# A two-block transformer step with 32 routed experts on one core: the experts' biases split into three bfloat16 parts over 128 partitions, and the gated part normalised later

## The chip, the core and the metric

The kernel runs on one core of a Trainium2 chip. A core has TensorE (matmuls, PE in the profile; its weight loads are PEld), VectorE (DVE), ScalarE (ACT), GpSimd (POOL) and SyncE (SP), which issues most of the loads from DRAM; 16 DMA engines move the data. ScalarE and GpSimd issue some loads too, in line with their other instructions. The metric is the device time of one execution in microseconds (us), the median of three runs, lower is better. [...]

## The reference

256 tokens of width 1024 go through two blocks. The first block mixes tokens (windowed attention beside a gated part), then routes each token to 4 of 32 experts; the second block mixes again and has a feed-forward part. What the change touches, cut down:

```python
def chunked_spatial_gating(u, g, ln_g, ln_b, w_s, b_s):
    u = gelu(u)
    g = layer_norm(gelu(g))            # per token and group of 64
    mixed = einsum('gts,bcsgd->bctgd', tril(w_s), g) + b_s
    return u * mixed
def token_mixer(...):
    q, k, v, u, g = split(x @ w_in + b_in)
    return concat([attention(q, k, v), chunked_spatial_gating(u, g, ...)]) @ w_out + b_out
def expert_block(xb, e):               # for each of 32 experts e
    gt = minimum(xb @ w_gate[e] + b_gate[e], 7)
    up = clip(xb @ w_up[e] + b_up[e], -7, 7)
    hid = gt * sigmoid(1.702 * gt) * (up + 1)
    return hid @ w_down[e] + b_down[e]
```

All data are float32. The gate, up and down weights of one expert are 1024 x 1024 each, so the experts have 402.7 MB of weights in all.

## The kernel before

The order of the instructions on each engine is the order in which the Python code writes them; each engine works through its own list and waits on semaphores.

`front` does the first block's mixer for two tiles of 128 tokens and the router. Its products are made from float32 values split into two parts (`pieces` and `pump` load a piece of a weight, cast its high part on ScalarE and subtract the low part on VectorE or GpSimd, by the letters of `FRONT_LOW`). The order on TensorE is: k, v and q; `scores` (attention scores, softmax on VectorE and ScalarE); four `gate_half` for the gated input; `trp(0)` (transposes of the softmaxed scores of group 0, which `normalise(0)` has divided by their sums: the half s=0 on VectorE, the half s=1 on GpSimd); the chunk `u_chunk(0)`; `trp(1)`, `trp(2)`; `u_chunk(1)` to `u_chunk(3)`, each of which fills one of three accumulator banks tagged `mm` and is evicted through an activation on ScalarE; then `pv` (scores times values, three times, into the same three banks), the gating product, and the output projection (`out_half`, columns 0 to 511 as `wo0` for both tiles in four slices, then `wo1`). The gated input is evicted into `gx`, its statistics go through VectorE, and it is normalised: tile 0 by two VectorE instructions, tile 1 by eight ScalarE activations of 64 columns. `cc` and `cb` fold the norm's bias into the router's logits: `cc` is copied out of two columns of small products, and one more small product makes `cb` of it.

`moe` works in capacity 64: an expert has 64 slots of gathered tokens, and experts go in pairs (`EB` = 2). `gate_up(e)` forms `pg` and `pu`, `[128, 512]` each: rows 0 to 63 are the 64 slots by output columns 0 to 511, rows 64 to 127 the same slots by columns 512 to 1023. So each matmul uses 64 of the array's 128 columns, and the two column halves are written alternately. The bias opens the accumulation as a product of its own: a column of the identity, broadcast to 64 columns, against `bgu`, in which the 32 gate biases lie on partitions 0 to 31 and the up biases on 32 to 63, so with 32 rows of the array, in float32:

```python
r = slice(32 * q, 32 * q + 32)
self.mm(p[64 * fh:64 * fh + 64, :], self.ident[r, 32 * q + e:32 * q + e + 1].to_broadcast([32, CAP]),
        self.bgu[r, fh * 512:(fh + 1) * 512], start=True, stop=False)
```

`product` then adds eight slices of 128 rows for both halves. `finish` runs the down product of the expert before. The weights come through nine buffers (`PAIRS`) of 2 MB, each half of one weight matrix; `fetch` issues the load into a buffer behind the product that read it last, and 18 loads of 1 MB are issued in the front already. At a pair's end TensorE transposes the gated one-hot `og`, which VectorE makes in `gates_of`.

Of the kernel before, what the change touches and what calls it, by code (L numbers as in the profile page):

```python
# [12 lines left out]
F32 = mybir.dt.float32  # L13
F32R = mybir.dt.float32r
BF = mybir.dt.bfloat16
I32 = mybir.dt.int32
AF = mybir.ActivationFunctionType
# [54 lines left out]
class Net:  # L72
# [66 lines left out]
    def run(self):  # L139
        nc, tc, ctx, a = self.nc, self.tc, self.ctx, self.a  # L140
        ctx.enter_context(tc.manual_schedule())
        self.cpool = ctx.enter_context(tc.tile_pool(name="consts", bufs=1))
        cp = self.cpool
        pa = self.pa = ctx.enter_context(tc.tile_pool(name="ring_a", bufs=1))
        bctx = ctx.enter_context(ExitStack())
        pb = self.pb = bctx.enter_context(tc.tile_pool(name="ring_b", bufs=1))

        self.x = cp.tile([128, NT, D], F32, name="x")
        for t in range(NT):
            nc.sync.dma_start(self.x[:, t, :], a["x"][0, t * 128:(t + 1) * 128, :])  # L150

        self.ident = cp.tile([128, 128], F32, name="ident")
        make_identity(nc, self.ident)
        self.h = cp.tile([128, NT, D], F32, name="h")
        self.lg = cp.tile([128, NT, NE], F32, name="lg")
        self.bgu = pb.tile([64, D], F32, name="bgu")

        self.ones = pb.tile([128, 96], F32, name="ones")
        nc.gpsimd.memset(self.ones, 1.0)
        self.bits = pb.tile([128, 2, 128], BF, name="bits")  # L160
        nc.gpsimd.memset(self.bits, 1.0)
        nc.gpsimd.affine_select(out=self.bits[:, 0], in_=self.bits[:, 0], compare_op=OP.is_ge, fill=0.0, base=-1,
                                pattern=[[1, 128]], channel_multiplier=-1)
        self.slot1 = pb.tile([128, CAP], F32, name="slot1")
        nc.gpsimd.iota(self.slot1, pattern=[[1, CAP]], base=1, channel_multiplier=0,
                       allow_small_or_imprecise_dtypes=True)
        self.top = pb.tile([128, NT, 8], F32, name="top")

        self.norm1 = pb.tile([128, 2, KC], F32, name="norm1")
        with ExitStack() as fctx:  # L170
            self.front(fctx)
        if self.stop == "front":
            return
        self.acc, self.h = self.h, self.x
        self.late = ctx.enter_context(tc.tile_pool(name="late", bufs=1, side="right", reuse_waits="tile"))
        with ExitStack() as mctx:
            sums = self.moe(mctx)
            if self.stop == "moe":
                for t in range(NT):
                    for n in range(2):  # L180
                        nc.vector.tensor_copy(self.acc[:, t, n * 512:(n + 1) * 512], sums[t][n])
                self.dump("acc", self.acc)
                return
            self.tail_norm(sums)
        bctx.close()
        with ExitStack() as tctx:
            self.mixer2(tctx)
        if self.stop == "mixer2":
            return
        self.ffn2()  # L190
# [9 lines left out]
    def front(self, fctx):  # L200
        nc, tc, a = self.nc, self.tc, self.a
        V, S, G = nc.vector, nc.scalar, nc.gpsimd
        fp = fctx.enter_context(tc.tile_pool(name="front", bufs=1))
        f2 = fctx.enter_context(tc.tile_pool(name="front2", bufs=2))
        ps = fctx.enter_context(tc.tile_pool(name="front_ps", bufs=1, space=PSUM, reuse_waits="tile"))

        def bank(tag, shape):
            return ps.tile(shape, F32, tag=tag, bufs={"mm": 3, "s": 4, "o": 1}[tag], name=self.nm(tag))
# [82 lines left out]
        def after_wo():  # L291
            L["wr"] = load("wr", [128, KC, NE], a["w_router"][0].rearrange("(k p) e -> p k e", p=128))
            L["br"] = load("br", [128, NE], bcast_rows(a["b_router"], NE))
            for q, nme in enumerate(("b_gate", "b_up")):
                nc.sync.dma_start(self.bgu[32 * q:32 * q + 32, :], a[nme][0])

        self.pieces(spec, halves, [slot[f"r{i}"] for i in range(9)])
        self.after = {0: after_kv, 2: after_q, 4: after_g, 7: after_wo}
# [165 lines left out]
        def u_chunk(c):  # L464
            S.activation(uT[:, c, :], channels("u"), AF.Gelu_apprx_tanh, bias=bqs[:, 6 + c:7 + c])

        for i in range(3):
            scores(i)

        r = self.h  # L470
        for t in range(NT):
            for n in range(2):
                ns = slice(n * 512, (n + 1) * 512)
                V.scalar_tensor_tensor(r[:, t, ns], self.x[:, t, ns], ALPHA, L["bout"][:, ns], op0=OP.mult, op1=OP.add)

        p = bank("s", [128, 4, 128])
        for gg in range(8):
# [25 lines left out]
        rs = self.rsqrt(fp, mv[:, :, 1], 16, add=1e-5)  # L503
        nb = fp.tile([128, 8], F32, name="gnb")
        V.scalar_tensor_tensor(nb, mv[:, 8:16, 0], -1.0, rs[:, 8:16], op0=OP.mult, op1=OP.mult)
        for j in range(8):
            S.activation(g[:, 8 + j, :], g[:, 8 + j, :], AF.Identity, scale=rs[:, 8 + j:9 + j], bias=nb[:, j:j + 1])
        gt = g[:, 0:8]
        V.tensor_tensor(gt, gt, mv[:, 0:8, 0:1].to_broadcast([128, 8, 64]), op=OP.subtract)
        V.tensor_tensor(gt, gt, rs[:, 0:8, None].to_broadcast([128, 8, 64]), op=OP.mult)  # L510

        u_chunk(1)
        u_chunk(2)
        u_chunk(3)
        xp = part_tiles()
        for i in range(3):
# [92 lines left out]
        for i in range(4):  # L609
            out_half(po, range(NT), i, self.parts("wo0"))  # L610
            freed()
        for t in range(NT):
            evict(t, 0, po[t])
        cc = fp.tile([128, 2], F32, name="cc")
        V.tensor_copy(cc[:, 0:1], by_experts("b", wr, lambda k: bqs[:, 10 + k:11 + k], 1))
        V.tensor_copy(cc[:, 1:2], by_experts("m", wrg, lambda k: self.ones[:, 0:1], 1))
        fac = {}
        p = bank("mm", [128, 512])
        for i in range(4):
            out_half({0: p}, (0,), i, self.parts("wo1", i))  # L620
            if i == 0:
                pc = bank("s", [128, 2, NE])
                for x in range(2):
                    self.mm(pc[:, x, :], cc[:, x:x + 1].to_broadcast([128, 128]), ist)
                V.tensor_tensor(cb[:, 0, :], pc[:, 0, :], L["br"], op=OP.add)
                V.tensor_copy(cb[:, 1, :], pc[:, 1, :])
            elif i > 1:
                turned(i - 2, 0, 4)
        evict(0, 1, p)
        fac[0] = norm(0)  # L630
# [76 lines left out]
    def moe(self, mctx):  # L707
# [141 lines left out]
        def gate_up(e, between=()):  # L849
            b, el = divmod(e, EB)  # L850
            pg, pu = bank("g", 2, [128, 512]), bank("u", 2, [128, 512])
            for q, (p, nme) in enumerate(((pg, "w_gate"), (pu, "w_up"))):
                for fh in range(2):
                    r = slice(32 * q, 32 * q + 32)
                    self.mm(p[64 * fh:64 * fh + 64, :], self.ident[r, 32 * q + e:32 * q + e + 1].to_broadcast([32, CAP]),
                            self.bgu[r, fh * 512:(fh + 1) * 512], start=True, stop=False)
                product(p, lambda k: xg[b][:, k, el * CAP:(el + 1) * CAP], weights_of(e, nme), False)
                for f in between if not q else ():
                    f()
            return swiglu(pg, pu)  # L860
# [1228 lines left out]
```

## Time and profile before

| | |
|---|---|
| median of three runs | 1596.21 us (1593.58 to 1598.78) |
| the profiled execution | 1599.51 us |
| its span, first to last instruction | 1597.9 us |
| mean granted clock | 0.962 |
| busy: TensorE, VectorE, ScalarE, GpSimd | 1491.1, 612.0, 374.6, 143.8 us |
| read from DRAM | 486.78 MB |

Busy times are unions of the instructions' spans. A float32 matmul leaves two records on TensorE, one for each half of its work; records overlap since matmuls are pipelined. An instruction's name gives the tile written, an arrow, and the tiles read. Line L89 is the helper that all matmuls go through, L1355 and L1356 the split of the weights.

### The profile page before, as it was taken

Reading aid. Unit: us, or ns where it says so; the run is one execution under the profiler, and the core shown is the slowest. Engines: PE = TensorE matmul, PEld = TensorE weight load, DVE = VectorE, ACT = ScalarE, POOL = GpSimd, SP = SyncE. Lnnn points to the kernel's source line nnn. Section 1 sums busy time; section 2 is a strip of 40 time slices with the busy share of each in tenths; the row PEclk is TensorE's granted clock in tenths of the full one; section 3 lists DMA queues with packets and bytes.
Section 4 is the critical chain, followed back from the end, with each engine's and each line's share of the span. In section 5 each row is a group of like instructions: output and inputs, shape, how many; then the busy total and the mean of one; then the engine's idle time right before and its main releaser. Section 6 shows DMA issues by size and latency. Waiting matters only on the chain. (4 is left out here: it accounts for less than half of the span.)

```text
span 1597.9 us, 19498 instructions
## 1 busy us (share of the span) xinstructions
PE 1491.1 (93%) x8102; PEld 832.1 (52%) x8102; DVE 612.0 (38%) x1138; ACT 374.6 (23%) x644; POOL 143.8 (9%) x140
## 2 busy tenths in 40 slices
PE   8889899999999998999999999997988899999998
PEld 7773233332332333332333333334877787799998
DVE  5852231221221212121211421215568556776664
ACT  4531110110101101111101111102634223355552
POOL 2200000000000002000000000003444214200000
PEclk9999889999999999999999999998999999999999
DMA  9769989999999999999999999981433124665540
GB/s 300 269 272 391 410 326 381 401 428 404 399 429 402 399 429 389 413 425 404 403 417 428 428 427 428 426 326 59 159 112 116 30 76 143 208 240 187 191 153 27
DMA packets 94482, 489.59 MB, mean 306 GB/s; under 512 B 14105, under 2 KB 44521, under 8 KB 67255
## 3 DMA queue, kind: packets, MB, share of 16 engines
q1 hardware_dynamic: 92768, 486.91, 76.3%
q8 instruction: 65, 1.06, 0.3%
q0 software_dynamic: 672, 0.72, 0.2%
q10 hardware_dynamic: 950, 0.69, 0.1%
q14 instruction: 27, 0.21, 0.0%
HBM read 486.78 MB, written 1.51 MB: 306 GB/s over the span
## 5 line engine op out<-in xcount | busy, mean ns | idle before, releaser
L89 PE MATMUL g<-w,xg 128*64 128x512 f32 x1024 | 251.4, 648 | 0.0
L89 PE MATMUL y<-w,hidT 128*64 128x512 f32 x1024 | 226.1, 594 | 1.1 <-ACT hidT L836 1.1
L89 PE MATMUL u<-w,xg 128*64 128x512 f32 x1024 | 226.8, 595 | 0.0
L89 PEld LDWEIGHTS g<-w,xg 128*64 128x64 f32 x1024 | 76.2, 149 | 180.0 <-issue 178.9
L1355 ACT CAST w<-w 128x1024 fp32r<-128x1024 f32 (+1 forms) x116 | 118.6, 1035 | 149.5 <-PE pj L89 66.8
L89 PEld LDWEIGHTS u<-w,xg 128*64 128x64 f32 x1024 | 70.7, 137 | 153.9 <-issue 153.6
L89 PEld LDWEIGHTS y<-w,hidT 128*64 128x64 f32 x1024 | 71.9, 137 | 148.9 <-issue 147.3
L1356 DVE TENSOR_TENSOR w<-w,w 128x1024 fp32r<-128x1024 f32 x83 | 106.8, 1302 | 85.6 <-ACT w L1355 85.5
L1356 POOL TENSOR_TENSOR w<-w,w 128x1024 fp32r<-128x1024 f32 (+1 forms) x33 | 79.2, 2405 | 598.8 <-ACT w L1355 587.6
L844 ACT COPY y<-y 64x512 f32<-64x512 f32 x64 | 37.1, 580 | 374.6 <-PE y L89 374.2
L822 DVE TENSOR_SCALAR g<-g 128x512 f32<-128x512 f32 x32 | 22.1, 691 | 257.2 <-PE g L89 257.2
L837 DVE COPY hidT<-tr 128x256 f32<-128x256 f32 x32 | 13.6, 425 | 229.4 <-ACT hidT L836 229.4
L825 DVE TENSOR_SCALAR g<-u 128x512 f32<-128x512 f32 x32 | 22.1, 692 | 185.8 <-PE u L89 185.8
L823 ACT ACTIVATE sg<-g 128x512 f32<-128x512 f32 x32 | 20.1, 630 | 287.1 <-DVE g L822 287.1
L89 PE MATMUL pj<-w,h2p 128*128 128x512 f32 x336 | 83.1, 403 | 1.9 <-DVE w L1356 1.9
L89 PE MATMUL sc<-y,ogT 128*128 128x512 f32 x124 | 62.5, 619 | 11.7 <-DVE h L793 10.3
L89 PEld LDWEIGHTS pj<-w,h2p 128*128 128x128 f32 x336 | 62.9, 191 | 18.4 <-DVE w L1356 2.7
L793 DVE TENSOR_TENSOR h<-h,sc 128x512 f32<-128x512 f32 x60 | 41.0, 686 | 33.4 <-PE sc L89 31.8
L1356 DVE TENSOR_TENSOR wp<-w,wp 128x1024 fp32r<-128x1024 f32 x32 | 38.4, 1223 | 18.6 <-ACT wp L1355 18.6
L767 ACT ACTIVATE xg<-tr,norm 128x128 f32<-128x128 f32 x32 | 12.9, 454 | 138.3 <-DVE xg L765 136.4
L89 PEld LDWEIGHTS sc<-y,ogT 128*128 128x128 f32 x124 | 20.0, 189 | 45.6 <-DVE h L793 32.8
L89 PE MATMUL g<-bgu,ident 32*64 32x512 f32 x128 | 42.1, 739 | 0.0
(540 smaller groups left out, 1877.5 us busy)
## 6 DMA issues: line engine op xcount, KB each, us to landing
w<-in_w_up_dram SPq DMA_DIRECT2D x58, 2048.0 KB, 9.9
w<-in_w_down_dram SPq DMA_DIRECT2D x58, 2048.0 KB, 13.8
w<-in_w_gate_dram SPq DMA_DIRECT2D x56, 2048.0 KB, 13.5
w<-in_w_in_dram SPq DMA_DIRECT2D x27, 1024.0 KB, 5.0
w<-in_w_ffn_up_dram SPq DMA_DIRECT2D x22, 1024.0 KB, 5.2
w<-in_w_gate_dram SPq DMA_DIRECT2D x16, 1024.0 KB, 9.8
w<-in_w_up_dram SPq DMA_DIRECT2D x12, 1024.0 KB, 7.4
w<-in_w_down_dram SPq DMA_DIRECT2D x12, 1024.0 KB, 11.7
```

Source lines behind the costliest of these rows:

```text
L89: return self.nc.tensor.matmul(out, lhsT, rhs, start=start, stop=stop)
L767: nc.scalar.activation(o, p, AF.Identity, scale=g, bias=b)
L793: nc.vector.tensor_tensor(dst, dst, pp[dh], op=OP.add)
L822: nc.vector.tensor_scalar(g1, pg, 7.0, None, op0=OP.min)
L823: nc.scalar.activation(sg, g1, AF.Sigmoid, scale=1.702)
L825: nc.vector.tensor_scalar(g1, pu, -7.0, 7.0, op0=OP.max, op1=OP.min)
L837: nc.vector.tensor_copy(hidT[:, 2:4].rearrange("p j f s -> p j (f s)"), p[:, 2:4])
L844: nc.scalar.copy(yv[64 * i:64 * i + 64, hf * 512:(hf + 1) * 512], py[64 * hf:64 * hf + 64, :])
L1355: nc.scalar.copy(t[:, 0], src)
L1356: self.low[j % len(self.low)].tensor_tensor(t[:, 1], src, t[:, 0].bitcast(F32), op=OP.subtract)
```

## The change

There are two separate parts and one more move in the code.

The biases: `bgu` becomes a bfloat16 tile of 128 partitions and 2048 columns, 32 experts on partitions 0 to 31 (first part), again on 32 to 63 (second part) and 64 to 95 (third part); partitions 96 to 127 are cleared. Its columns are the gate bias and the up bias of an expert side by side. `ohb` holds the identity of 32 three times below each other, so a column of it, broadcast to 64 columns, picks the three parts of one expert and adds them in the accumulator. To make the parts, the biases are loaded as 128 rows of 512 (`bf`), and ScalarE and VectorE cast and subtract in turn. The three parts `bp` go to a DRAM tensor `bd` and come back in the other shape by three loads; all four transfers are issued by GpSimd.

The gated part: the eight activations that normalise tile 1 move behind the eviction of `u_chunk(2)`. And the small products for `cc` and `cb` move from behind the output projection's first half into it.

```diff
-        self.bgu = pb.tile([64, D], F32, name="bgu")
+        self.bgu = pb.tile([128, 2 * D], BF, name="bgu")
+        self.ohb = pb.tile([128, NE], BF, name="ohb")
+        nc.gpsimd.memset(self.bgu[96:128], 0.0)
+        nc.gpsimd.memset(self.ohb, 0.0)
...
-            for q, nme in enumerate(("b_gate", "b_up")):
-                nc.sync.dma_start(self.bgu[32 * q:32 * q + 32, :], a[nme][0])
+            L["bf"] = fp.tile([128, 512], F32, name="bf")
+            for j in range(4):
+                nc.sync.dma_start(L["bf"][j::4, :], a[("b_gate", "b_up")[j // 2]][0][:, j % 2 * 512:j % 2 * 512 + 512])
...
         r = self.h
+        bf, bp = L["bf"], fp.tile([128, 3, 512], BF, name="bp")
         for t in range(NT):
+            S.copy(bp[:, t], bf)
             for n in range(2):
                 ns = slice(n * 512, (n + 1) * 512)
                 V.scalar_tensor_tensor(r[:, t, ns], self.x[:, t, ns], ALPHA, L["bout"][:, ns], op0=OP.mult, op1=OP.add)
+            V.tensor_tensor(bf, bf, bp[:, t], op=OP.subtract)
+        S.copy(bp[:, 2], bf)
+        bd = dr.tile([NE, 4, 3, 512], BF, name="bd")
+        G.dma_start(bd.rearrange("e j s c -> (e j) s c"), bp)
+        for s in range(3):
+            G.tensor_copy(self.ohb[32 * s:32 * s + 32], self.ident[32 * s:32 * s + 32, 32 * s:32 * s + 32])
+            G.dma_start(self.bgu[32 * s:32 * s + 32, :].rearrange("e (j c) -> e j c", j=4), bd[:, :, s, :])
...
-        for j in range(8):
-            S.activation(g[:, 8 + j, :], g[:, 8 + j, :], AF.Identity, scale=rs[:, 8 + j:9 + j], bias=nb[:, j:j + 1])
...
         u_chunk(1)
         u_chunk(2)
+        for j in range(8):
+            S.activation(g[:, 8 + j, :], g[:, 8 + j, :], AF.Identity, scale=rs[:, 8 + j:9 + j], bias=nb[:, j:j + 1])
         u_chunk(3)
...
         for i in range(4):
             out_half(po, range(NT), i, self.parts("wo0"))
             freed()
-        for t in range(NT):
-            evict(t, 0, po[t])
-        cc = fp.tile([128, 2], F32, name="cc")
-        V.tensor_copy(cc[:, 0:1], by_experts("b", wr, lambda k: bqs[:, 10 + k:11 + k], 1))
-        V.tensor_copy(cc[:, 1:2], by_experts("m", wrg, lambda k: self.ones[:, 0:1], 1))
+            if i == 1:
+                cc = fp.tile([128, 2], F32, name="cc")
+                V.tensor_copy(cc[:, 0:1], by_experts("b", wr, lambda k: bqs[:, 10 + k:11 + k], 1))
+                V.tensor_copy(cc[:, 1:2], by_experts("m", wrg, lambda k: self.ones[:, 0:1], 1))
+            elif i == 3:
                 pc = bank("s", [128, 2, NE])
                 for x in range(2):
                     self.mm(pc[:, x, :], cc[:, x:x + 1].to_broadcast([128, 128]), ist)
...
+        for t in range(NT):
+            evict(t, 0, po[t])
...
-                    r = slice(32 * q, 32 * q + 32)
-                    self.mm(p[64 * fh:64 * fh + 64, :], self.ident[r, 32 * q + e:32 * q + e + 1].to_broadcast([32, CAP]),
-                            self.bgu[r, fh * 512:(fh + 1) * 512], start=True, stop=False)
+                    self.mm(p[64 * fh:64 * fh + 64, :], self.ohb[:, e:e + 1].to_broadcast([128, CAP]),
+                            self.bgu[:, (2 * q + fh) * 512:(2 * q + fh + 1) * 512], start=True, stop=False)
```

On GpSimd, in the front between the scores and the chunks of u, these rows stand before the change (`w_113<-w_113,st` is the softmax normalising of a group, `w_116` and `w_117` on the left of the others are the low parts of weight slices):

```order
L1356 TENSOR_TENSOR w_116<-w_109,w_116 128x1024
L1356 TENSOR_TENSOR w_117<-w_110,w_117 128x1024
L426 TENSOR_TENSOR w_113<-w_113,st_411 128x512
L1356 TENSOR_TENSOR w_116<-w_110,w_116 128x1024
L426 TENSOR_TENSOR w_113<-w_113,st_434 128x512
L426 TENSOR_TENSOR w_112<-w_112,st_453 128x512
```

and these at the same place after it:

```order
L1371 TENSOR_TENSOR w_122<-w_115,w_122 128x1024
L486 DMA bd<-bp 128x1536
L488 CAST ohb<-ident 32x32
L489 DMA bgu<-bd 32x4x512
L488 CAST ohb<-ident 32x32
L489 DMA bgu<-bd 32x4x512
L488 CAST ohb<-ident 32x32
L489 DMA bgu<-bd 32x4x512
L431 TENSOR_TENSOR w_118<-w_118,st_419 128x512
L1371 TENSOR_TENSOR w_121<-w_115,w_121 128x1024
```

The store of the parts, three casts and three loads now stand ahead of the first softmax normalising; the first of the loads waits for the store to land.

On ScalarE, from the eviction of `u_chunk(0)` on, before (`mm` are the chunks' banks, `gnb` marks the normalising of `gx`, `L1355` casts a weight slice):

```order
L465 ACTIVATE w_114<-mm_605,bqs 128x256
L438 COPY w_113<-s_639 128x512
L438 COPY w_112<-s_651 128x512
L507 ACTIVATE w_113<-w_113,gnb,rsi_658 128x64 x8
L1355 CAST w_116<-w_111 128x1024
L465 ACTIVATE w_114<-mm_683,bqs 128x256
L1355 CAST w_117<-w_112 128x1024
L465 ACTIVATE w_114<-mm_712,bqs 128x256
L1355 CAST w_117<-w_112 128x1024
L465 ACTIVATE w_114<-mm_740,bqs 128x256
```

and after:

```order
L470 ACTIVATE w_119<-mm_627,bqs 128x256
L443 COPY w_118<-s_661 128x512
L443 COPY w_117<-s_673 128x512
L1370 CAST w_121<-w_116 128x1024
L470 ACTIVATE w_119<-mm_697,bqs 128x256
L1370 CAST w_122<-w_117 128x1024
L470 ACTIVATE w_119<-mm_726,bqs 128x256
L528 ACTIVATE w_118<-w_118,gnb,rsi_680 128x64 x8
L1370 CAST w_122<-w_117 128x1024
L470 ACTIVATE w_119<-mm_762,bqs 128x256
```

The eight activations stood ahead of the evictions of chunks 1 to 3 and stand ahead of chunk 3's alone now.

On TensorE, in the third expert, before (`g` and `u` are the banks `pg` and `pu`):

```order
L89 MATMUL g_1412<-bgu,ident 64x512 x2
L89 MATMUL g_1412<-w_110,xg_1338 64x512 x8
L89 MATMUL g_1412<-w_111,xg_1338 64x512 x8
L89 MATMUL u_1413<-bgu,ident 64x512 x2
L89 MATMUL u_1413<-w_112,xg_1338 64x512 x8
```

and after:

```order
L89 LDWEIGHTS ohb
L89 MATMUL g_1435<-bgu,ohb 64x512
L89 LDWEIGHTS ohb
L89 MATMUL g_1435<-bgu,ohb 64x512
L89 MATMUL g_1435<-w_115,xg_1361 64x512 x8
L89 MATMUL g_1435<-w_116,xg_1361 64x512 x8
L89 LDWEIGHTS ohb
L89 MATMUL u_1436<-bgu,ohb 64x512
```

A bfloat16 matmul has its weight load as an instruction of its own in the program, a float32 matmul has it within; the number and the place of the bias matmuls are the same.

## Rows read from the trace of the kernel before

**Rows 1.** Two stretches: us, busy us of each engine, PEclk, DMA share, GB/s.

```profile
117.93:1078.53 960.60, 909.51 (x4069) 321.42 (x4068) 206.93 (x395) 99.94 (x207) 14.66 (x48) 0.96 0.97 404
0.00:117.93 117.93, 102.41 (x769) 90.88 (x769) 75.89 (x188) 56.16 (x106) 22.14 (x28) 0.94 0.81 285
```

**Rows 2.** TensorE's waits, 110 to 1062: us in total, times, longest.

```profile
PE tr L93 <- DVE og L814: 29.4, 15, 2.0
```

**Rows 3.** The sync queue's waits, 300 to 1060, its two largest.

```profile
SPq L700 <- PE g L89: 264.8, 50, 16.1
SPq L700 <- PE y L89: 240.4, 48, 11.6
```

**Rows 4.** Two pairs of experts as stretches, columns as in rows 1.

```profile
484.29:545.64 61.35, 58.55 (x259) 20.54 (x258) 12.00 (x20) 6.31 (x13) 0.00 (x0) 0.94 0.98 411
...
970.02:1028.03 58.01, 55.21 (x259) 19.99 (x258) 12.00 (x20) 6.31 (x13) 0.00 (x0) 1.00 1.01 428
```

**Rows 5.** TensorE in order of time from 499 on: start, us, what, records.

```profile
499.71 4.03 PE L89 MATMUL u<-w,xg 128*64 128x512 f32 x18
503.58 7.04 PE L89 MATMUL y<-w,hidT 128*64 128x512 f32 x32
...
511.13 1.07 PE L89 MATMUL g<-bgu,ident 32*64 32x512 f32 x4
512.13 7.09 PE L89 MATMUL g<-w,xg 128*64 128x512 f32 x32
519.15 1.07 PE L89 MATMUL u<-bgu,ident 32*64 32x512 f32 x4
520.15 7.09 PE L89 MATMUL u<-w,xg 128*64 128x512 f32 x32
527.17 2.05 PE L89 MATMUL tr<-oh,x 128*128 128x128 f32 x16
```

**Rows 6.** TensorE in order of time, around the router's bfloat16 products.

```profile
113.10 0.23 PE L89 MATMUL u<-sel,bits 128*128 128x32 bf16 x3
113.17 1.14 PE L89 MATMUL y<-ident 128*128 128x128 f32 x8
```

**Rows 7.** DMA issues, whole run, last row 970 to 1028: KB, us to landing.

```profile
lng<-in_ln_g_dram POOLq DMA_DIRECT2D x2, 256.0 KB, 10.5
l_rank<-rkT POOLq DMA_DIRECT2D x1, 32.0 KB, 3.0
...
w<-in_w_down_dram SPq DMA_DIRECT2D x4, 2048.0 KB, 18.9
```

**Rows 8.** TensorE in order of time: the last expert's down product.

```profile
1083.00 7.09 PE L89 MATMUL y<-w,hidT 128*64 128x512 f32 x32
```

**Rows 9.** TensorE in order of time in the front, with the waits.

```profile
50.85 1.03 PE L93 MATMUL s<-ident,w 128*128 128x128 f32 x8
...
69.96 5.21 PE L89 MATMUL mm<-w,w 128*64 128x128 f32 x48 [4.31 <-ACT w L465]
...
93.34 0.63 PE L89 MATMUL s<-ist,cc 128*128 128x32 f32 x4 [3.27 <-DVE cc L615]
```

**Rows 10.** ScalarE in order of time in the front.

```profile
44.66 0.19 ACT L417 ACTIVATE st<-st 128x4 f32<-128x4 f32 x1
...
65.84 2.76 ACT L507 ACTIVATE w<-w,gnb,rsi 128x64 f32<-128x64 f32 x8 [5.14 <-DVE gnb L505]
...
69.44 0.47 ACT L465 ACTIVATE w<-mm,bqs 128x256 f32<-128x256 f32 x1
...
72.42 0.57 ACT L325 CAST xp<-mm 128x512 fp32r<-128x512 f32 x1
```

**Rows 11.** GpSimd in order of time in the front.

```profile
20.99 2.41 POOL L1356 TENSOR_TENSOR w<-w,w 128x1024 fp32r<-128x1024 f32 x1 [16.02 <-ACT w L1355]
...
47.74 1.48 POOL L426 TENSOR_TENSOR w<-w,st 128x512 f32<-128x512 f32 x1 [12.97 <-DVE st L424]
```

**Rows 12.** One stretch of the front, columns as in rows 1.

```profile
42.00:57.00 15.00, 14.21 (x87) 12.35 (x86) 14.72 (x25) 7.94 (x15) 8.95 (x5) 1.00 1.02 407
```

More of the change, by code (lines that the diff above doesn't have):

```diff
@@ L204, in front @@
         f2 = fctx.enter_context(tc.tile_pool(name="front2", bufs=2))
+        dr = fctx.enter_context(tc.tile_pool(name="front_dr", bufs=1, space=bass.MemoryType.DRAM))
         ps = fctx.enter_context(tc.tile_pool(name="front_ps", bufs=1, space=PSUM, reuse_waits="tile"))
@@ L611, in front @@
             freed()
-        for t in range(NT):
-            evict(t, 0, po[t])
-        cc = fp.tile([128, 2], F32, name="cc")
-        V.tensor_copy(cc[:, 0:1], by_experts("b", wr, lambda k: bqs[:, 10 + k:11 + k], 1))
-        V.tensor_copy(cc[:, 1:2], by_experts("m", wrg, lambda k: self.ones[:, 0:1], 1))
[L617 to L621, printed above, removed]
+            if i == 1:
[3 more added lines that the diff above has]
+            elif i == 3:
                 pc = bank("s", [128, 2, NE])
@@ L626, in front @@
                 V.tensor_copy(cb[:, 1, :], pc[:, 1, :])
-            elif i > 1:
+        for t in range(NT):
+            evict(t, 0, po[t])
+        fac = {}
+        p = bank("mm", [128, 512])
+        for i in range(4):
+            out_half({0: p}, (0,), i, self.parts("wo1", i))
+            if i > 1:
                 turned(i - 2, 0, 4)
```

## The prediction, made before the changed kernel had run

> **What bounds the kernel now.** I read the stretches first: 117.9 of the 1597.9 us are the front (mixer, router, first gather), the next 960.6 the experts but for the last product, in which TensorE is busy for 909.5 and DMA for 97% of the time [rows 1]. Two engines so near their limit leave open which one binds, so I went to TensorE's waits in the experts' part. None of them names a DMA; the largest is 29.4 us for the gated one-hot, 15 times 2 us, once per pair of experts [rows 2]. The sync queue's waits say the same from the other side: between 300 and 1060 its loads stood 505 us waiting for the gate and down products alone to let go of a buffer [rows 3]. So TensorE binds. But DMA is close behind: two pairs of experts, at 484 and at 970, have the same instructions and take 61.35 and 58.01 us; in the slower one the granted clock is 0.94 and DMA's share 0.98, in the faster one 1.00 and 1.01 at 428 GB/s [rows 4]. A pair needs 12 loads of 2048 KB, 25.2 MB, and 25.2 MB at 428 GB/s is 58.8 us: without a drop of the clock TensorE is already a little faster than the loads.
>
> **The bias products.** One expert's rows [rows 5]: 18 records of the up product run from 499.71 to 503.58, where the down product follows without a gap. The two column halves run side by side, so that is 9 pairs of records at 0.430 us. A float32 matmul leaves two records and streams its 512 columns twice in each, so one pass for both halves takes 0.215 us and a product of 16 pairs of records 6.88 us. The bias takes two pairs of records: 512.13 - 511.13 = 1.00 us. From one bias to the next product's end there are 8.02 us (511.13 to 519.15, and 519.15 to 527.17), of which 6.88 + 0.86 = 7.74 are streaming. The other 0.28 lies where 32x64 follows 128x64, 128x64 follows 32x64 and 128x64 is left for 128x128, some 0.1 each, and nothing is lost between two products of 128x64.
>
> After the change a bias is one bfloat16 pass over 128 rows: 0.215 us if the halves still overlap. Then a gate or up product with its bias takes 7.15 to 7.2 us (0.215 + 6.88 + one change of shape) and saves 0.85, if going from bfloat16 to float32 costs nothing. If that costs what a change of shape costs, the saving is 1.00 - 0.215 - 0.05 = 0.74. If the two halves run one after the other, 0.43 in all, it is 0.57 or a little more. The trace has one place where bfloat16 stands between float32 matmuls: three start at 113.10 and the next float32 ones at 113.17 [rows 6]. That is no visible toll, but on small matmuls, so I take 0.80: 64 products (32 experts, two each) x 0.80 = **-51 us**, with -36 and -55 as ends. [...]
>
> **What DMA gives back.** A pair without a drop would take 58.0 - 4 x 0.80 = 54.8 us, 4.0 less than its loads. The cushion: nine buffers of one load each, twelve loads a pair, so a load is issued when its buffer is let go and needed eight loads later, 8/12 x 58.0 = 38.7 us; late in the experts' part the slowest land 18.9 us after issue [rows 7], which leaves some 20 us. So DMA does not stop TensorE at once; a run of five pairs without a drop uses the cushion up, and a pair with a drop (58.2) takes hardly any. I take **+3 us** (0 to 12). The floor: of 32 x 12.6 MB, 18.9 MB are loaded ahead, and 383.8 MB at 428 GB/s from 121 us last until 1018. The last half product, which needs the last load, starts at about 1086.5 now (half way through the row from 1083.00 on [rows 8]); less 3 us, the least that any load took to land [rows 7], the gain of the experts' part cannot pass 65 us, and hardly 60.
>
> **The clock.** 0.96 over 960.6 us [rows 1] is 38 us lost. [...] The pairs keep the wait and get shorter, so which of them drop will change. The ends are none (-38, which the floor cuts) and all (+16). I take **0**.
>
> **The front.** *Removed waits:* PV's first matmul stood 4.31 us until the second gated chunk's eviction freed a bank; the eviction (69.44) stood behind eight normalising activations, 2.76 us from 65.84 [rows 9, 10]. With these behind chunk 2's eviction, PV follows chunk 3 directly: -4.3. And 3.27 us in which TensorE waits for cc [rows 9]: now computed after the second slice of the output weights and read after the fourth: -3.3.
>
> *Added:* three casts on ScalarE and two subtractions on VectorE that wait for each other in turn. A 128x512 cast takes 0.57 [rows 10], so the last part is ready about 3.5 us after the exponentials end (44.85 [rows 10]): 48.5. Then GpSimd issues the store to DRAM and, behind its landing, three loads with a small cast each. All four stand ahead of the softmax normalising that GpSimd did at 47.74 [rows 11], and ahead of the low parts of the second and fourth slice of u. How long the store takes no row shows: 32 KB through this queue landed after 3.0 us with DMA free, 256 KB after 10.5 with DMA full [rows 7]. Between 42 and 57 DMA is full, 1.02 [rows 12], so I take 9: 57.5. Three issues at 0.55 and casts, 2.3; normalising ends at 61.3 in place of 49.2. The transposes that need it are the second half of eight from 50.85 on [rows 9], so TensorE stands about 10 us there (bounds 4 to 13). GpSimd's chain behind it is as late as TensorE, so little is added. The low clock that lies on PV now (5.21 us for 48 short matmuls [rows 9]) falls on the chunk behind the new stall instead, so that is even. Net +10 - 4.3 - 3.3 = **+2 us** (-4 to +6). [...]
>
> The rest costs nothing: the clearing of the two new tiles at the start is covered by GpSimd's 16 us of idleness before 20.99 [rows 11] (uncovered perhaps 2 us); two more issues on the sync queue, some 0.9 us, are covered by the loads queued there; the eight activations have until the gating, 5 us later.
>
> **Sum.** -51 + 3 + 0 + 2 = -46. The profiled execution took 1599.5 us, its span 1597.9, the median of the runs is 1596.2; 1599.5 - 46 = 1553.5, and beside the median **1550 us**.
>
> **Rivals.** (1) *The halves do not overlap*: 64 x 0.57 = 36 and, with DMA out of the way, +2 in front: 1562. For it: bfloat16 weights come as an instruction of their own; against it: the float32 halves do overlap, 18 records in 3.87 us. (2) *Loads bind in the stretches with full clock*: if the cushion is gone before the last 10 experts, those gain nothing, 22/32 x 51 = 35: 1563. Against it: the 20 us. (3) *Every pair drops*: +16, no DMA term: 1563. [...] (4) *No pair drops*: the floor, 60 us, front +2: 1538. (5) *Slower*: the change of type on TensorE drains the array. There are two changes per product, 128 in all, and the gain of 51 is gone at 0.40 us each, slower above it; at 0.5 it is +13: 1609. Against it the start 0.07 us after [rows 6], but for that place alone. (6) *The detour through DRAM costs what the biases save*: GpSimd would have to be held 55 us, and DMA is empty long before.
>
> **How the numbers follow.** Chances: forecast 0.58, (1) 0.10, (2) 0.07, (3) 0.12, (4) 0.10, (5) 0.02, others 0.01. Cases (1) to (3) end at 1562 or 1563, (4) at 1538; with the front's -4 and +6 the range is 1533 to 1567. It leaves out the halves in sequence together with all drops, and the floor with the quick store. Within 0.3% (5 us) of before is about what a measurement cannot tell from no change; only (5) comes near. Faster 0.97, same 0.01, slower 0.02.
>
> **What would show it.** Right: from a bias's first record to its product's end about 7.2 us where 8.02 stood; full-clock pairs near 54.8 us; a wait of TensorE for GpSimd's normalising of 4 to 13 us near 52, none for cc, none for an eviction at PV. Wrong: bias records starting 0.2 us apart; waits for a weight load of over 12 us in the experts' part; a clock mean under 0.94 there; a first expert that starts over 6 us later than 117.9.

## The result and the profile after

The changed kernel takes **1546.6 us** (median of 4 runs, 1542.4 to 1548.5) where the kernel before takes 1595.7 (4 runs); the ratio is 0.9687, 95% interval 0.9661 to 0.9714. The profiled execution is the fastest of the four, 1542.44 us, and that of before, 1599.51, took longer than any of its four here, so the two traces are 57 us apart and the medians 49. In the traces the front is 1.6 us shorter, the experts' part (first bias product to the end of the last down product, 972.2 us before by [rows 1, 8]) 50.0, and the rest 5.5. The change leaves the code of that rest as it was; in the 13 traces of this case it took 502.1 to 510.0 us, so its 5.5 us cannot be put down to the change.

Stretches of the changed kernel: us, busy us of each engine, PEclk (the granted share of TensorE's clock, 1.00 at its fullest; the clock records of this trace and of that of before read 1 or 0.5 and nothing else), DMA share, GB/s. They answer to [rows 1, 4].

```profile
0.00:116.38 116.38, 98.97 (x769) 87.54 (x769) 71.34 (x190) 57.84 (x109) 25.50 (x37) 0.96 0.83 295
116.38:1038.56 922.18, 853.53 (x3985) 317.72 (x3984) 207.09 (x396) 101.48 (x209) 14.46 (x48) 0.97 1.00 421
228.76:284.96 56.20, 53.40 (x253) 20.02 (x252) 11.99 (x20) 6.31 (x13) 0.00 (x0) 0.97 0.98 411
448.45:502.95 54.50, 51.70 (x253) 19.57 (x252) 11.99 (x20) 6.32 (x13) 0.00 (x0) 1.00 1.01 427
797.98:856.72 58.74, 53.84 (x252) 19.87 (x252) 21.33 (x74) 6.31 (x13) 0.00 (x0) 0.97 1.01 428
```

DMA is now full through the whole part (1.00). A pair at full clock takes 54.50 us in place of 58.01, one with a drop of the clock and no wait for weights 56.20; a late pair takes 58.74, which is the time of its 25.2 MB at 428 GB/s.

TensorE's waits, 116 to 1040 (us in total, times, longest), beside [rows 2]:

```profile
PE tr L93 <- DVE og L830: 29.4, 15, 2.0
PE u L89 <- DMA w<-in_w_up_dram: 12.4, 11, 1.3
PE sc L89 <- DVE h L809: 10.3, 14, 0.8
PE tr L89 <- PEq L936: 5.8, 1, 5.8
...
PE g L89 <- DMA w<-in_w_gate_dram: 1.4, 2, 1.0
```

Waits for weights, of which before had none, come to 13.8 us. The first stand at expert 15, behind ten experts (5 to 14) in which the clock never drops; from expert 23 on every pair has some.

TensorE in order of time, beside [rows 5]:

```profile
470.19 0.41 PE L89 MATMUL g<-bgu,ohb 128*64 128x512 bf16 x2
470.43 7.03 PE L89 MATMUL g<-w,xg 128*64 128x512 f32 x32
477.29 0.38 PE L89 MATMUL u<-bgu,ohb 128*64 128x512 bf16 x2
477.51 7.03 PE L89 MATMUL u<-w,xg 128*64 128x512 f32 x32
484.47 2.05 PE L89 MATMUL tr<-oh,x 128*128 128x128 f32 x16
```

From bias to product 0.24 and 0.22 us, where it was 1.00; from one bias to the product's end 7.10 and 7.18, where it was 8.02. The halves overlap, and the change of type costs nothing that can be seen.

In the front, TensorE's two new waits (same columns, 0 to 118), and GpSimd in order of time, beside [rows 9, 11]:

```profile
PE s L93 <- POOL w L431: 6.7, 1, 6.7
PE s L93 <- DVE st L428: 2.5, 1, 2.5
```

```profile
47.72 0.77 POOL L486 DMA_DIRECT2D bd<-bp  x1 [14.07 <-ACT bp L484]
48.50 1.18 POOL L488 CAST ohb<-ident 32x32 bf16<-32x32 f32 x1
54.89 0.59 POOL L489 DMA_DIRECT2D bgu<-bd  x1 [5.22 <-DMA bd<-bp]
...
56.42 0.55 POOL L489 DMA_DIRECT2D bgu<-bd  x1
57.04 1.04 POOL L431 TENSOR_TENSOR w<-w,st 128x512 f32<-128x512 f32 x1
```

The normalising that TensorE needs from 50.85 us on in before (it started at 47.74 there) now starts at 57.04, behind the detour. The wait for `cc` is gone and that at PV (values) is 0.7 us.

DMA issues of the whole run (KB, us to landing), beside [rows 7]:

```profile
w<-in_w_up_dram SPq DMA_DIRECT2D x58, 2048.0 KB, 30.6
w<-in_w_down_dram SPq DMA_DIRECT2D x58, 2048.0 KB, 32.2
...
bd<-bp POOLq DMA_DIRECT2D x1, 384.0 KB, 6.9
```

In before the medians of the weight loads were 9.9 and 13.8 us. A load that waits 30 us in full queues has used most of the 39 us between its issue and its use.

### The profile page after: what moved, and what is told of

It reads as the page before. It is cut to its first block, busy times and chain, and to the rows that moved or that the text cites. A ratio compares the mean times of both kernels' runs of the same rounds, so it can differ in the third digit from the quotient of the medians.

```text
span 1540.8 us, 19267 instructions
## 1 busy us (share of the span) xinstructions
PE 1417.2 (92%) x7974; PEld 817.8 (53%) x7974; DVE 604.0 (39%) x1140; ACT 376.5 (24%) x647; POOL 146.9 (10%) x149
## 5 line engine op out<-in xcount | busy, mean ns | idle before, releaser
L89 PE MATMUL g<-w,xg 128*64 128x512 f32 x1024 | 242.0, 628 | 1.4 <-DMA w<-in_w_gate_dram 1.4
L853 DVE COPY hidT<-tr 128x256 f32<-128x256 f32 x32 | 13.6, 424 | 228.5 <-ACT hidT L852 228.5
L89 PEld LDWEIGHTS tr<-oh,x 128*128 128x128 f32 x256 | 31.4, 200 | 18.0 <-issue 17.9
```

Of the source, the lines that this page charges most:

```text
L89: return self.nc.tensor.matmul(out, lhsT, rhs, start=start, stop=stop)
L853: nc.vector.tensor_copy(hidT[:, 2:4].rearrange("p j f s -> p j (f s)"), p[:, 2:4])
```

## The experiments

**Theory**: the bias edit makes TensorE fast enough that the loads bind, so a part of what it saves, and of what the clock gives, comes back as waits for weights. **Rival A**: TensorE still binds, and each us taken off it comes off the time. **Rival B**, for the front: the detour through DRAM is what its stall comes from, and it can be had for nothing elsewhere.

| run | time, us (median) | ratio to before, 95% | experts from, us | experts' part, us | lost to low clock in it |
|---|---|---|---|---|---|
| before (profiled) | 1595.7 | 1 | 117.9 | 972.2 | 37.5 |
| the change | 1546.6 | 0.9687 (0.9661, 0.9714) | 116.4 | 922.2 | 23.9 |
| e1_moves_only | 1589.5 | 0.9961 (0.9933, 0.9989) | 109.2 | 971.1 | 35.8 |
| e2_bias_only | 1552.5 | 0.9716 (0.9698, 0.9735) | 124.1 | 921.7 | 23.9 |
| e3_late_detour | 1541.0 | 0.9643 (0.9624, 0.9661) | 114.9 | 918.6 | 18.8 |
| e4_f32_128rows | 1567.8 | 0.9815 (0.9797, 0.9833) | 118.3 | 939.3 | 18.8 |
| e5_bf16_32rows | 1545.1 | 0.9675 (0.966, 0.969) | 116.9 | 916.3 | 20.5 |
| e6_no_bias | 1546.1 | 0.969 (0.9674, 0.9707) | 117.9 | 917.0 | 18.8 |
| e7_early_gates | 1546.2 | 0.9689 (0.9674, 0.9704) | 116.4 | 920.2 | 10.2 |
| e8_split_on_pool | 1544.0 | 0.9663 (0.9647, 0.968) | 115.2 | 921.0 | 23.9 |
| e9_split_late | 1541.3 | 0.9661 (0.9638, 0.9685) | 112.2 | 921.6 | 22.2 |
| e10_before_early_gates | 1556.0 | 0.9766 (0.9732, 0.98) | 118.1 | 927.0 | 11.9 |
| e11_later_start | 1545.9 | 0.9669 (0.9641, 0.9697) | 117.8 | 920.7 | 22.2 |

The last column is summed over the clock's records in each trace: the length of a record times what the granted clock lacked to 1. Each run was compared with runs of before on the same chip, so times of different runs are best set side by side by their ratios.

**The two halves apart.** e1 is before with the two moves in the front (the eight activations behind chunk 2, `cc` and `cb` into the output projection); e2 is the changed kernel with these undone.

```diff
 e1, against before (e2: the reverse, against the change)
-        for j in range(8):
-            S.activation(g[:, 8 + j, :], g[:, 8 + j, :], AF.Identity, scale=rs[:, 8 + j:9 + j], bias=nb[:, j:j + 1])
...
+        for j in range(8):
+            S.activation(g[:, 8 + j, :], g[:, 8 + j, :], AF.Identity, scale=rs[:, 8 + j:9 + j], bias=nb[:, j:j + 1])
...
+            if i == 1:
+                cc = fp.tile([128, 2], F32, name="cc")
...
+            elif i == 3:
+                pc = bank("s", [128, 2, NE])
...
```

> The kernel before with the two moves alone (the eight activations behind the second chunk's eviction, cc and cb inside the output projection's first half), biases as before. My theory: TensorE's two waits of 4.3 and 3.3 us go, and the stretch of low clock on the value products may go with the first; 1585 to 1589 us, experts starting 7 to 11 us earlier than 117.9, a pair of experts at full clock still 58.0. Rival, the wait only moves to the gating product, which then waits for the activations: no more than 4 us earlier, 1592 or so.

> The changed kernel with both moves undone, so the biases' part alone. My theory: the detour's stall of some 9 us in the front stays, cc's 3.3 us wait and 2 to 3 us at the value products come back; experts start at 121 to 123 and a pair at full clock takes 54.5; 1551 to 1554 us. Rival, since loads bind in the second half of the experts' part, a later start of TensorE is swallowed there: within 2 us of the changed kernel's 1546.6.

The two savings, 6.9 us (against the median of before beside these runs, 1596.4) and 43.9, add up to 50.8, about the whole. The moves alone start the experts 8.8 us earlier. Of that 3.3 are the wait for `cc` and 1.9 that at PV, where 2.4 stay. The rest, 3.6, goes along with the clock, which in that trace is full from the start to there (1.00, in before 0.94); that the moves bring the full clock is not shown, since no other front here has it:

```profile
0.00:109.16 109.16, 97.60 (x769) 86.15 (x769) 74.47 (x188) 56.03 (x106) 22.07 (x28) 1.00 0.86 308
```

e1's time is 0.5 us over my range. In e2 the wait for `cc` is back (3.3), that at PV is not (0.4, where I had 2 to 3), and the experts start 1.1 us later than I had allowed.

**Type and shape apart.** e4 is before with a bias of 128 rows of the array, zeros in 64 of them, in float32; e5 is before with one bfloat16 part on 32 rows.

```diff
 e4
-        self.bgu = pb.tile([64, D], F32, name="bgu")
+        self.bgu = pb.tile([128, D], F32, name="bgu")
+        nc.gpsimd.memset(self.bgu[64:128], 0.0)
...
+                    self.mm(p[64 * fh:64 * fh + 64, :], self.ident[:, 32 * q + e:32 * q + e + 1].to_broadcast([128, CAP]),
+                            self.bgu[:, fh * 512:(fh + 1) * 512], start=True, stop=False)
 e5
-                    self.mm(p[64 * fh:64 * fh + 64, :], self.ident[r, 32 * q + e:32 * q + e + 1].to_broadcast([32, CAP]),
-                            self.bgu[r, fh * 512:(fh + 1) * 512], start=True, stop=False)
+                    self.mm(p[64 * fh:64 * fh + 64, :], self.ohb[r, 32 * q + e:32 * q + e + 1].to_broadcast([32, CAP]),
+                            self.bgh[r, fh * 512:(fh + 1) * 512], start=True, stop=False)
```

> The kernel before with float32 biases still, but read as 128 rows (rows 64 to 127 cleared), so that the bias product has the array shape of the products around it. It tells the change of shape from the change of type. My theory: a bias stays at 4 records of float32 but the tolls of 0.1 us at the changes of shape go; a pair at full clock 57.3 to 57.7, in all 5 to 11 us less than before apart from the clock, 1585 to 1591. Rival, the shape costs nothing and the gap comes from the bias's own records: 58.0 and no change, 1596.

> The kernel before with the bias products alone changed: one bfloat16 part on the 32 rows of before, so the type changes and the array shape does not (the biases are rounded to bfloat16: two of their three parts are left out). If type and shape each have a price of their own, the type's is 0.877 - 0.22 = 0.655 us per product, and a pair at full clock takes 58.01 - 4 x 0.655 = 55.4 us. If the gain of 0.877 needs both together, the pair stays above 56.5; if the shape costs nothing behind a bfloat16 product, it falls to 54.5. The time lies between that of the changed kernel and that of the run with float32 on 128 rows, 1547 to 1568, since late pairs wait for weights in any case; I expect 1555.

A pair at full clock, in e4 and in e5 (columns as above):

```profile
235.54:292.66 57.12, 54.32 (x259) 20.55 (x258) 12.00 (x20) 6.31 (x13) 0.00 (x0) 1.00 1.00 420
```

```profile
748.17:803.50 55.33, 52.53 (x253) 19.67 (x252) 11.99 (x20) 6.30 (x13) 0.00 (x0) 1.00 1.01 430
```

Per product the shape is worth (58.01 - 57.12) / 4 = 0.22 us and the type (58.01 - 55.33) / 4 = 0.67. Together 0.89; the change has (58.01 - 54.50) / 4 = 0.88. So they add. e4 came out 17 us below my range: its part is 32.9 us shorter than that of before, 14 by the price and 18.7 by the clock, which I had set aside. My time for e5 was 10 us too high: at 55.33 a pair TensorE uses the cushion up only at the very end (0.8 us of waits for weights), and its part is the shortest of all, 916.3, while that of the change, with less work for TensorE, takes 922.2. Both have DMA full (1.01), but from 240 to 560 and from 640 to 1000 us it moved 430 GB/s in e5 and 428 and 427 in the change; over 900 us that makes 5 us, an estimate. So TensorE's work does not order the two, and the loads can. Why their rate differs no run shows.

**Does TensorE still bind?** e6 leaves the bias products out of the changed kernel; e7 computes the gated one-hot before the pair's second gate product and transposes it before the down product.

```diff
 e6
-                for fh in range(2):
-                    self.mm(p[64 * fh:64 * fh + 64, :], self.ohb[:, e:e + 1].to_broadcast([128, CAP]),
-                            self.bgu[:, (2 * q + fh) * 512:(2 * q + fh + 1) * 512], start=True, stop=False)
-                product(p, lambda k: xg[b][:, k, el * CAP:(el + 1) * CAP], weights_of(e, nme), False)
+                product(p, lambda k: xg[b][:, k, el * CAP:(el + 1) * CAP], weights_of(e, nme), True)
 e7 (e10: the same on before)
+            list(early or ())
             down(hidT.pop(e), weights_of(e, "w_down"), y[b], el)
...
+                if e > 1:
+                    early = gates_of(b)
+                    next(early)
...
-                finish(e - 1)
+                finish(e - 1, early)
...
-            if b:
+            if b and not early:
                 list(gates_of(b))
```

> The changed kernel without its 64 gate and up bias products (the biases are left out). TensorE saves 64 x 0.24 = 15 us more. If the loads bind in the experts' part, the part (922.2) gets only 2 to 8 us shorter, the waits for weights (13.8) grow to 20 or more, and the pairs from 740 on stay at 58 to 60 us; time 1538 to 1546. If TensorE binds, the part gets 15 us shorter with the waits as they were: 1531.

> The changed kernel with the gated one-hot computed before an expert pair's second gate product and transposed before the down product, in 13 of the 15 places where TensorE waits 2.0 us for it. TensorE is rid of up to 26 us of waits. If the loads bind, most of it comes back as waits for weights (13.8 becomes 30 or more), the experts' part is 910 to 920 us and the time 1537 to 1545. If TensorE binds, the part gets some 26 us shorter, about 896, time 1521. On the clock: if the drops of the late pairs belong to this 2 us wait, they go (the part's loss of 23.9 us falls under 8); if they belong to any wait, those for weights, they stay.

Neither gains in time, 1546.1 and 1546.2 us (for e6 at the upper end of my range, for e7 1 us over it). The part of e6 and then that of e7, as stretches:

```profile
117.91:1034.95 917.04, 839.76 (x3857) 312.18 (x3856) 207.15 (x396) 101.47 (x209) 14.44 (x48) 0.98 1.00 423
```

```profile
116.39:1036.53 920.14, 846.72 (x3985) 316.64 (x3984) 208.29 (x396) 101.39 (x209) 14.43 (x48) 0.99 1.00 422
```

TensorE's waits in them, again e6 and then e7:

```profile
PE u L89 <- DMA w<-in_w_up_dram: 19.5, 16, 1.2
...
PE g L89 <- DMA w<-in_w_gate_dram: 6.9, 10, 1.5
```

```profile
PE u L89 <- DMA w<-in_w_up_dram: 20.8, 18, 2.5
PE y L89 <- DMA w<-in_w_down_dram: 12.6, 13, 1.3
PE g L89 <- DMA w<-in_w_gate_dram: 11.0, 14, 1.3
...
PE tr L93 <- DVE og L830: 3.2, 2, 2.0
```

In e6 TensorE is busy 13.8 us less than in the change and idle 8.6 us more (its waits for weights rose from 13.8 to 26.4), so the part is 5.2 us shorter. In e7 26.2 us of waits for the one-hot went, 13.7 of low clock too (of which 6.8 show in TensorE's busy time, 846.7 against 853.5), and the waits for weights rose from 13.8 to 44.4; the part is 2 us shorter. Of two late pairs, one in the change (797.98, above) and the same one here, the first runs at 0.97 and the second at 1.00, and they take 58.74 and 58.73:

```profile
278.72:331.01 52.29, 51.51 (x253) 19.71 (x252) 12.09 (x20) 6.32 (x14) 0.00 (x0) 1.00 1.01 428
793.78:852.51 58.73, 52.83 (x253) 19.60 (x252) 21.45 (x74) 6.32 (x14) 0.00 (x0) 1.00 1.01 427
```

An early pair shows what TensorE could do, 52.29. That settles it against rival A.

**The same edit on before.**

> The kernel before, biases in float32 as they were, with the gated one-hot computed and transposed earlier in 13 of 15 places. If TensorE bound the experts of before and the drops of the clock belong to the 2 us wait, the part (972.2) loses 13 x 2.0 = 26 us of waits and 20 to 30 us of its 37.5 us of low clock, that is to 916 to 928, where the loads bind: time 1540 to 1555, as much as the change itself gives without touching a bias. If the drops belong to something else, only the 26 us come off: 946, 1570. If loads bound before already, under 5 us come off: 1592.

```profile
290.85:346.65 55.80, 55.02 (x259) 20.08 (x259) 12.09 (x20) 6.30 (x14) 0.00 (x0) 1.00 1.01 428
118.06:1045.04 926.98, 895.61 (x4113) 322.47 (x4112) 208.39 (x396) 101.24 (x210) 14.61 (x48) 0.99 0.99 419
```

Before, TensorE did bind: here the edit takes 45 us off the part, 26 of waits and 25.6 of low clock, less 6.9 that come back as waits for weights. In the pairs from the third on, where the 2 us wait is gone, the clock does not drop once outside the stretch around the branch (537 to 637), here and in e7; the waits for weights in e7, most of 1.0 to 1.3 us and one of 2.5, do not bring a drop there. So a drop goes with the wait for the one-hot, and not with every wait as long; why, no run shows. Both ways to relieve TensorE, this one and the bias, end near the same part, 916 to 927 us (the time of e10, 1556.0, is 1 us over my range).

**The front.** e3 issues the store and the loads behind the softmax normalising; e8 puts the split on GpSimd too, there; e9 puts all of that behind the last low part of u.

```diff
 e3: the store and the loads, from behind the split to ahead of trp(0), on GpSimd behind normalise(2)
-        bd = dr.tile([NE, 4, 3, 512], BF, name="bd")
-        G.dma_start(bd.rearrange("e j s c -> (e j) s c"), bp)
...
         gate_half(pg, 3)
+        bd = dr.tile([NE, 4, 3, 512], BF, name="bd")
+        G.dma_start(bd.rearrange("e j s c -> (e j) s c"), bp)
...
 e8: the same place for this; e9: this behind u_chunk(3)
-            S.copy(bp[:, t], bf)
...
-            V.tensor_tensor(bf, bf, bp[:, t], op=OP.subtract)
-        S.copy(bp[:, 2], bf)
...
+        for t in range(NT):
+            G.tensor_copy(bp[:, t], bf)
+            G.tensor_tensor(bf, bf, bp[:, t], op=OP.subtract)
+        G.tensor_copy(bp[:, 2], bf)
+        bd = dr.tile([NE, 4, 3, 512], BF, name="bd")
+        G.dma_start(bd.rearrange("e j s c -> (e j) s c"), bp)
...
```

> The changed kernel with GpSimd's store, casts and three loads placed behind the last softmax normalising, nothing else. My theory: the two waits of 2.5 and 6.7 us around 50 to 58 us shrink to under 2, experts start some 7 us earlier (about 109), and since the stream of loads starts earlier with them the whole is 1538 to 1541. Rival, the loads bind and the front's gain is spent waiting for them: experts start earlier but TensorE waits for weights 5 to 8 us more than the 13.8 now, 1546.

> The changed kernel with the whole split (three casts and two subtractions) on GpSimd, behind the softmax normalising, and the store and loads behind that. If the front's stall comes from the split standing ahead of the normalising on VectorE, ScalarE and GpSimd, the waits of 6.7 for GpSimd and 2.5 for VectorE go and PV's wait stays under 1 us: the experts start 6 to 9 us earlier, at 107 to 110, where the run with the late store had won 1.5 and lost 2.4 at PV. If the loads bind the end, half of it or more is given back there: 1538 to 1545 in all; if not, 1538.

> The changed kernel with the whole split on GpSimd and the detour through DRAM put behind the last low part of u that GpSimd computes. In the run with the split behind the softmax normalising, that low part stood behind the loads from DRAM and PV waited 4.0 us for it; here it stands ahead of them, so the front should be that of the moves alone: no wait for GpSimd in it, experts from 109 to 111 us on (116.4 in the changed kernel). As the experts' part is 916 to 922 us in all six runs with a bfloat16 bias, counted from its own start, the 6 us of the front come off the end in full: 1537 to 1541. If loads set an absolute end, whatever the start, the experts' last product still ends at 1033 or later: 1541 to 1545.

Each run took the stall named in its expectation away and showed the next one. In e3 the wait for GpSimd fell to 0.2, but 2.5 for VectorE (which still did the subtractions first) stayed, and at PV 2.4 stood where the change has 0.7; in e8 PV waited for the low part of u, which stood behind the loads; in e9, no wait for GpSimd or for the subtractions is left:

```profile
PE mm L89 <- POOL w L1372: 4.0, 1, 4.0
```

```profile
PE mm L89 <- ACT w L470: 3.0, 1, 3.0
...
PE s L93 <- DVE w L443: 0.8, 1, 0.8
```

(the first from e8, the two from e9, 36 to 120). The experts of e9 start 4.2 us earlier than those of the change and end 4.7 earlier (1033.8 against 1038.6), so a gain in the front is not given back. Of rival B the first half holds: with the detour late, no wait for it is left. The second holds in part: of the 9.2 us of the two waits 4.2 are won. e9 missed the 109 of e1 by 3 us: the mean clock of its front is 0.95 (e1 1.00), and PV waits 3.0 for ScalarE. All three runs started the experts later than I had expected (109, 107 to 110, 109 to 111). e3 and e9 are the fastest, some 5 us under the change; their intervals (0.9624 to 0.9661, 0.9638 to 0.9685) still touch or overlap the change's.

**A later start.** e11 has 7 more warming matmuls ahead of the experts.

```diff
-WARM = 12, 10, 11, 14, 4
+WARM = 12, 10, 11, 21, 4
```

> The changed kernel with 7 more warming matmuls on TensorE just ahead of the experts, some 1.7 us in all; nothing else. Two questions. If the loads bind the experts' part and their stream stands until the first expert lets go of a buffer, the part starts at about 118.1 and ends 1.7 us later too, at 1040 (922 us long, time 1548); if the loads set an absolute end, it ends at 1038 as before. And TensorE's wait of 5.8 us at the branch behind the sixteenth expert, which the kernels with bfloat16 biases have and the four with float32 biases or none have not (0.3 us): if it comes from the full DMA queues alone it stays at 5.7 to 6.2; if it depends on where the branch lies in TensorE's instruction stream, which 7 instructions more shift, it goes or changes by over 1 us.

The start was 1.4 us later and the end 0.1 earlier, so over so short a shift this run cannot tell; e2 (7.8 later, end 7.3 later) and e9 can: the stream of loads moves with the first expert. The branch's wait stayed, 5.6 us. (Kernels without it were five, not four: before, e1, e4, e10 and e6.) The shift by 7 matmuls does not move it, and full queues alone do not make it, since e6 has them and there the branch takes 0.4 us.

The traces say more, in the DMA queue that the profile calls `instruction` (q8). It makes 65 reads of 16 KB in before, 64 in the change and 63 in e6, where TensorE has 16346, 16093 and 15836 records, 251 of them to a read in each of the three. In the five kernels that pass the branch at once a read starts 9 to 16 us ahead of it (in before at 597.2, the branch at 612.8). In the eight that are held the last one lies 33 to 39 us back (in the change 532.4 and 566.7), the next starts 3.3 to 3.9 us behind the branch's start (570.1), and in each of the eight TensorE goes on 1.5 us after that one has landed (571.1 and 572.7). So in these traces the hold ends with that read; that TensorE waits there for its instructions is my reading of the times, and no run tests it. Ahead of the branch before has 5673 records and e6 5419, the change 5548, e11 5576. At 251 records a read, an estimate from the three counts above, the bias edit moved the branch by half a read and leaving the biases out by a whole one; e11's 28 records are a ninth of one, and the wait stayed.

## Why the prediction was right, and where it was wrong

The forecast was 1550 and the measurement 1546.6, but two of its terms were wrong, by 14 and by 11 us, and largely cancelled: the clock gave 13.6 us where I had nothing, and waits for weights took 13.8 where I had 3. That the total fell 3 us from the forecast is in part luck.

*Bias products, -51.* The mechanism was right and the price a little low: 0.877 us each, 64 x 0.877 = 56.1, outside the upper end by 1 us. What I had put at 7.15 to 7.2 (bias and product) is 7.10 and 7.18, and the bfloat16 pass, put at 0.215, takes 0.24 and 0.22, about half of a pair of float32 records (7.03 / 16 = 0.44). The 0.1 us at each change of shape was read rightly: taking the changes away alone (e4) gives 0.22 per product. What I had left for the change of type, 0.05 each, is not there.

*DMA, +3.* This failed. The sentence was that a run of five pairs without a drop uses the cushion up and that a pair with a drop takes hardly any. The run came (experts 5 to 14), and the first wait for weights stands right behind it. But from expert 23 on every pair waits, though each of them has a drop: 54.5 us of work meet 58.8 us of loads, and even a pair with a drop (56.2) is shorter than its loads. I had 58.2 for that pair, because a drop cost 3.3 us in before [rows 4]; now it costs 1.7 (56.20 against 54.50). Waits for weights: 13.8 us. Rival (2) named this mechanism, with a chance of 0.07; e6 and e7 show it to be the bound. (By its own terms the range should start at 1596 - 60 - 4 = 1532, not 1533.)

*The clock, 0.* Lost time fell from 37.5 to 23.9 us, -13.6. The drops stand next to the 2 us wait, as e7 and e10 show (lost time 10.2 and 11.9 us with 13 of its 15 places gone). That as many drops would come was right: the part has 11 stretches of low clock in either trace, in 9 pairs of before (38 us at 3.3 a pair [rows 1, 4] would be 11 or 12) and in 10 of the change. What failed is the price of one: eight of the 11 last 6.8 us in before, nine of the 11 last 3.4 us in the change, and at the 0.5 that each of these records reads that is 3.4 and 1.7 us, beside 3.3 and 1.7 a pair. Why experts 5 to 14 have drops before and none after, with the same wait, I could not settle.

*The sum in the experts' part*: -56.1 - 13.6 + 13.8 + 5.8 at the branch - 1.9 (a wait that before had in that place) = -52.0; measured -50.0. TensorE's idle time did rise by what the last three terms say (68.7 against 51.1); its busy time fell by 67.5 us, not 69.7, and these two I cannot place. Where loads bind, these terms are not independent: e6 and e7 show that what is taken off TensorE there, by fewer products, fewer waits or a better clock, turns into waits for weights. So that the two errors cancelled has a reason too. The floor in the prediction, a gain of the part of 60 to 65 us, was too generous: it took 428 GB/s from 121 on; DMA moved 381 MB at 424 between 121 and 1020, by which the 383.8 MB last 8 us longer. The shortest part, that of e5, is 56 below that of before.

*The front, +2.* Measured -1.6. The waits of 3.3 for `cc` and, but for 0.7, of 4.3 at PV went as forecast. The stall for GpSimd was 6.7, where I said about 10: the store landed in 6.9 us, not 9. Not foreseen was VectorE, 2.5 (0.9 in e2 and e6, which have the same split there): the two subtractions stand ahead of the softmax sums on its queue, and I had costed them only as steps towards the store. The lower bound of the stall, 4, and with it the front's -4 (the quick store), no run shows: with the detour in this place the wait for GpSimd was 6.7 us in the change and e2, 6.6 in e6 and 6.4 in e11.

Of what the prediction had put down as signs of a wrong forecast one did appear, over 12 us of waits for weights.

## What to carry to other kernels

When two engines both sit within a few per cent of the bound, work out the floor that each sets for the whole part (here 384 MB of loads at 424 GB/s, 905 us and the two ends) and cap the sum of all terms by it, those in which you expect no gain too: price and clock together took TensorE past the floor, and the excess came back as waits. Test it by taking away something unrelated; if the time stays (e6, e7), the bound has moved, and a saving is to be sought in the bytes or in an earlier start of their stream (e9). For work that is moved into a queue, count not only what it needs but what stands behind it on each of its engines.

## What the runs showed of the hardware that I had not expected

- The compare-and-branch behind the sixteenth expert lasts 5.9 to 6.4 us on TensorE in the eight kernels with a bfloat16 bias (5.6 to 6.2 of them as TensorE's wait), and 0.35 to 0.45 us in the five others. In each of the eight it ends 1.5 us after the landing of a 16 KB read on the queue named `instruction` that starts 3.3 to 3.9 us behind the branch's start; in the five such a read stood 9 to 16 us ahead of it.
- The same 384 KB store landed in 2.9 us (e9, DMA share 0.43 meanwhile), 6.9 (the change, 1.03) and 8.2 (e3, 0.60), so the share alone does not set it.
- A drop of the clock cost a pair 3.3 us in before (low for 6.8 us) and 1.7 in the change (low for 3.4), beside the same wait of 2.0 us. A wait of 2.5 us for weights in e7 brought none.
